# Down projection of a SwiGLU block: eleven instead of seven of 22 weight pairs with seven products, their sums made earlier and kept in DRAM

## Chip, core and metric

The kernel runs on one core of one Trainium2 chip. The metric is the device time of one execution in microseconds (us), as a median of the runs shown. Engines are named as in the profile: PE (TensorE matmul), PEld (TensorE weight load), DVE (VectorE), ACT (ScalarE), POOL (GpSimd), SP (SyncE, which issues most DMAs; SPq is its queue).

## The reference, cut to what matters

A decoder block for 256 tokens (and 16 meta tokens) of width 2048, all in float32. RWKV-7 time mixing, forgetting attention, their gates and the output projection come first and are not touched by the change. What matters here is the feed-forward part at the end, with `w_gu` of 2048 x 11264 and `w_dn` of 5632 x 2048:

```python
    h = h + merged @ w_o
    gate, up = jnp.split(_rms(h, n2) @ w_gu, 2, axis=-1)
    return h + (jax.nn.silu(gate) * up) @ w_dn
```

## The kernel before

**Precision.** Every float32 operand is split into a high and a low part in a 32-bit matmul format: the high part is a rounded copy that ACT makes, the low part is the difference that DVE makes. A product of two operands is three matmuls (high x high, low x high, high x low; `product`, L1457 to L1463, each 512 columns wide). The split is `split` (L509) for activations and `wload` (L314) for weights, whose ACT line is L335 and DVE line L336.

**Weight tiles.** Weights come from DRAM by DMA on SP's queue into a tile `raw` of 128 x 1024 float32 (512 KB). ACT and DVE then make `wh` and `wl` of it. There are four buffers of each (`RAWB = 4`, `WB = 4`, L49 and L50). So a DMA can be issued as soon as DVE has read the tile four places earlier, and ACT can write `wh` as soon as PE has used the one four places earlier. `run` (L426) writes each tile's load ahead of the matmuls of the tile before it, so SP, ACT and DVE run ahead of PE as far as these buffers let them.

**Planner.** Small work beside the matmuls is written as generators. `spawn` sets one off, `slot` (L397) advances a clock of estimated PE time with every product, and when a generator's time has come its next step is put into the program there; the number that a step yields is the time until the next one in ns. That sets the program order. In this last part of the kernel the framework's scheduler may move instructions of an engine against each other by its own estimates; data dependencies are kept by semaphores.

**Gate and up** (L1386 to L1404). For each of eleven blocks of 512 columns, 8 weight tiles for the gate and 8 for up: 176 tiles, each used by 8 pairs of matmuls (one of 512 columns, L441, one of 256, L443 or L440). `hts` holds the normalized activations, high and low. `post_gate` and `post_up` finish a block on ACT and DVE and leave silu(gate) * up in `ach` and `acl` (high and low), with hidden units on the partitions.

**Down projection** (L1410 to L1573). The 5632 rows of `w_down` make 22 pairs of two 128-row blocks. The output is computed in two column groups (`cg`) of 1024 columns; within one, a pair is a 2 x 2 block product: two token halves, two row blocks, two column halves of 512.
- A slow pair (`slow_jobs`, L1469) has two weight tiles of 512 KB and makes eight products, four a tile, so 24 matmuls. They add up in four PSUM banks `dn`.
- A fast pair (`fast_jobs`, L1488) makes seven products (21 matmuls) in Winograd's form of Strassen's method. Three of them, and one more factor, need sums of token blocks (`sst`, made by `sums_of_pairs`, L1417, with ten DVE operations and four splits a batch), and four need differences of weight blocks (L1515: four DVE operations of 128 x 512 a fast pair and column group, into `tt`). It loads 1 MB into two `raw` tiles (`ra`, `rb`, L1496 and L1498) and makes four steps of weights: a half tile for one product, then three whole tiles for two products each. Four of its sums stay in PSUM banks `dnp` over all fast pairs; `sums_of_products` (L1547) adds them to the output once per column group, and `post` (L1555) adds `dn` and stores the output.
- `ORDER` (L71) says in which order pairs run. With F for a fast pair and S for a slow one it is eight S and then (F S) seven times in the first column group; S F S seven times and one S in the second.

SP's queue takes the weight loads in this order; there is no work for POOL in gate and up or in the down projection.

## Time and profile before

| | us |
|---|---|
| median of 3 runs (lowest to highest) | 1522.12 (1520.21 to 1522.53) |
| span of the profiled execution, first to last instruction | 1517.7 |
| gate and up, matmuls from 788.8 to 1278.1 | 489 |
| down projection, first to last start of its matmuls, 1278.3 to 1513.5 | 235 |
| from there to the end of the span | 4 |

The span is 4.4 us shorter than the median; what lies around it the profile does not show. In the profile, a line such as L1460 is a line of the kernel; a group of instructions has its count, its busy time, the mean of one, and the idle time of its engine just ahead with what ended it. PE's busy time is pipelined: a matmul of 512 columns lasts 0.39 us, but the next starts 0.23 us after it. So PE can look busy throughout although it waits now and then; waits show in the starts.

### The profile page before, as it was taken

Reading aid. Unit: us, or ns where it says so; the run is one execution under the profiler, and the core shown is the slowest. Engines: PE = TensorE matmul, PEld = TensorE weight load, DVE = VectorE, ACT = ScalarE, POOL = GpSimd, SP = SyncE. Lnnn points to the kernel's source line nnn. Section 1 sums busy time; section 2 is a strip of 40 time slices with the busy share of each in tenths; the row PEclk is TensorE's granted clock in tenths of the full one; section 3 lists DMA queues with packets and bytes.
Section 4 is the critical chain, followed back from the end, with each engine's and each line's share of the span. In section 5 each row is a group of like instructions: output and inputs, shape, how many; then the busy total and the mean of one; then the engine's idle time right before and its main releaser. Section 6 shows DMA issues by size and latency. Waiting matters only on the chain.

```text
span 1517.7 us, 26174 instructions
## 1 busy us (share of the span) xinstructions
PE 1509.9 (99%) x10071; PEld 1339.5 (88%) x10071; DVE 1112.0 (73%) x2009; ACT 808.3 (53%) x1230; POOL 99.3 (7%) x182
## 2 busy tenths in 40 slices
PE   9999999999999999999999999999999999999998
PEld 9999999999989888998888888888888888887887
DVE  7888699689789857875665666566566658879776
ACT  7664565475465545644554555454455545554543
POOL 2112202202202000000000000000000000000000
PEclk9999999999999999999999999999999999999999
DMA  8557456646645757777566666666666666566664
GB/s 271 166 166 212 119 156 185 170 122 173 188 127 149 223 152 214 234 231 240 181 179 192 189 187 193 191 186 192 190 187 191 193 186 182 178 211 201 213 206 138
DMA packets 210365, 283.32 MB, mean 187 GB/s; under 512 B 24320, under 2 KB 129296, under 8 KB 210240
## 3 DMA queue, kind: packets, MB, share of 16 engines
q1 hardware_dynamic: 205344, 277.25, 61.9%
q10 hardware_dynamic: 4896, 4.40, 0.9%
q8 instruction: 79, 1.29, 0.3%
q14 instruction: 46, 0.38, 0.1%
HBM read 274.36 MB, written 7.24 MB: 186 GB/s over the span
## 4 chain that ended last, share of the span: by engine, by line
PE 95%; DVE 3%; DMA 1%; issue 1%; ACT 0%; SPq 0%; DVEq 0%; ACTq 0%
PE up L441 11%; PE gt L441 11%; PE zg L441 8%; PE gt L443 5%; PE up L443 5%; PE dn L1461 4%; PE dn L1460 4%; PE dn L1462 4%; PE zg L443 4%; PE f L441 2%; PE br L365 2%; PE br L366 2%; PE br L367 2%; PE f L365 2%; PE wo L1329 2%; PE wo L1331 2%
## 5 line engine op out<-in xcount | busy, mean ns | idle before, releaser
L336 DVE TENSOR_TENSOR wl<-raw,wh 128x1024 fp32r<-128x1024 f32 x460 | 561.9, 1226 | 281.3 <-ACT wh L335 280.6
L335 ACT ACTIVATE wh<-raw 128x1024 fp32r<-128x1024 f32 x460 | 486.5, 1059 | 470.2 <-PE up L441 118.9
L441 PE MATMUL gt<-hts,wh 128*128 128x512 f32 x704 | 242.9, 393 | 0.0
L441 PE MATMUL up<-hts,wh 128*128 128x512 f32 x704 | 242.7, 392 | 0.0
L443 PE MATMUL gt<-hts,wl 128*128 128x256 f32 x660 | 184.8, 280 | 0.0
L443 PE MATMUL up<-hts,wl 128*128 128x256 f32 x660 | 184.6, 280 | 0.0
L441 PE MATMUL zg<-xhl,wh 128*128 128x512 f32 x512 | 181.2, 399 | 0.0
L441 PEld LDWEIGHTS up<-hts,wh 128*128 128x128 f32 x704 | 130.0, 188 | 25.2
L441 PEld LDWEIGHTS gt<-hts,wh 128*128 128x128 f32 x704 | 129.9, 188 | 25.1
L443 PE MATMUL zg<-xhl,wl 128*128 128x256 f32 x480 | 134.3, 280 | 0.0
L443 PEld LDWEIGHTS up<-hts,wl 128*128 128x128 f32 x660 | 125.3, 190 | 1.8
L443 PEld LDWEIGHTS gt<-hts,wl 128*128 128x128 f32 x660 | 125.3, 190 | 1.8
L441 PEld LDWEIGHTS zg<-xhl,wh 128*128 128x128 f32 x512 | 94.3, 188 | 18.7 <-issue 0.7
L1460 PE MATMUL dn<-wh,ach 128*128 128x512 f32 x282 | 110.7, 393 | 0.0
L1461 PE MATMUL dn<-wh,acl 128*128 128x512 f32 x282 | 110.6, 392 | 0.0
L1462 PE MATMUL dn<-wl,ach 128*128 128x512 f32 x282 | 110.5, 393 | 0.0
L443 PEld LDWEIGHTS zg<-xhl,wl 128*128 128x128 f32 x480 | 90.9, 189 | 1.2
L365 PE MATMUL f<-xhl,wh 128*128 128x272 f32 x256 | 75.9, 296 | 0.0
L367 PE MATMUL f<-xhl,wl 128*128 128x272 f32 x256 | 73.6, 288 | 0.0
L366 PE MATMUL f<-xhl,wh 128*128 128x272 f32 x256 | 73.6, 288 | 0.0
L1462 PEld LDWEIGHTS dn<-wl,ach 128*128 128x128 f32 x282 | 52.9, 187 | 12.3 <-DVE wl L336 0.3
L1461 PEld LDWEIGHTS dn<-wh,acl 128*128 128x128 f32 x282 | 52.9, 188 | 12.0
(493 smaller groups left out, 3056.7 us busy)
## 6 DMA issues: line engine op xcount, KB each, us to landing
raw<-in_w_gate_up_dram SPq DMA_DIRECT2D x176, 512.0 KB, 4.3
raw<-in_w_in_dram SPq DMA_DIRECT2D x160, 512.0 KB, 3.9
raw<-in_w_down_dram SPq DMA_DIRECT2D x74, 512.0 KB, 5.0
raw<-in_w_o_dram SPq DMA_DIRECT2D x32, 512.0 KB, 4.3
raw<-in_w_branch_a_dram SPq DMA_DIRECT2D x16, 512.0 KB, 4.6
raw<-in_w_branch_b_dram SPq DMA_DIRECT2D x16, 512.0 KB, 5.0
raw<-in_w_down_dram SPq DMA_DIRECT2D x28, 256.0 KB, 4.6
zgd<-zg ACTq DMA_DIRECT2D x30, 128.0 KB, 3.8
```

The lines of the kernel that those rows point to most:

```text
L335: nc.scalar.activation(th, rr, AF.Copy)
L336: nc.vector.tensor_tensor(tl, rr, th.bitcast(F32), op=ALU.subtract)
L365: nc.tensor.matmul(ps, wh, ah, start=first, stop=False)
L366: nc.tensor.matmul(ps, wh, al, start=False, stop=False)
L367: nc.tensor.matmul(ps, wl, ah, start=False, stop=last)
L441: nc.tensor.matmul(ps.rearrange("p (a t) -> p a t", a=2), wh, act, start=first, stop=last)
L443: nc.tensor.matmul(ps[:, :T], wl, act[:, 0, :], start=False, stop=False)
L1329: nc.tensor.matmul(o, ah[:, kt, ts_], hi, start=first, stop=False)
L1331: nc.tensor.matmul(o, ah[:, kt, ts_], lo_, start=False, stop=last)
L1460: nc.tensor.matmul(o, a[0], hi, start=first, stop=False)
L1461: nc.tensor.matmul(o, a[1], hi, start=False, stop=False)
L1462: nc.tensor.matmul(o, a[0], lo_, start=False, stop=last)
```

## The change

Eleven pairs (0 to 10) are fast instead of seven. What a fast pair needs beside the weights themselves is made during gate and up:

- `sums_of_weights`, a planned step that starts after the first gate block: for each of the 11 fast pairs and each column group, POOL issues two DMAs of 512 KB that load the pair's two row blocks into `r`; 8.5 us of planned time later DVE makes the four differences in three operations into `v` (one of 128 x 1024, two of 128 x 512), and POOL issues a DMA of 1 MB that stores them in a DRAM tile `ts`; 10.5 us later comes the next one.
- `sums_of_tokens`: at the end of an up block, for each fast pair, DVE makes the four token sums in four operations of 128 x 128, and POOL stores them in DRAM (256 KB).
- In the down projection, `split_of_sums` loads the token sums back (11 DMAs of 256 KB on POOL's queue) and splits them in six batches, two splits each.
- A fast pair's four weight steps are now four loads of their own on SP's queue: 256 KB, two of 256 KB, 512 KB of `ts`, 512 KB of `ts`. It uses four `raw` tiles (1.75 MB) where it used two (1 MB). The four DVE operations of L1515 and `sums_of_pairs` are gone.
- The order is S S S S, (F F S) five times, F S S in the first column group; S, (F F S) five times, F S S S S S in the second.
- For room in SBUF, `hts` is kept with all high parts ahead of all low parts, the output projection's small tiles move to a pool that is closed after the first gate block, and `finish_job` is called ahead of the down projection.

```diff
+HPART = KT * T + NMETA
+HTS = 2 * HPART
...
-FAST = [0, 1, 2, 3, 4, 5, 6]
-BATCHES = (2, 2, 2, 1)
-SLOW = list(range(7, 22))
-ORDER = [SLOW[:8] + [i for pair in zip(FAST, SLOW[8:]) for i in pair],
-         [i for n, f in enumerate(FAST) for i in (SLOW[2 * n], f, SLOW[2 * n + 1])] + SLOW[14:]]
+FAST = list(range(11))
+BATCHES = (2, 2, 2, 2, 2, 1)
+SLOW = list(range(11, 22))
+
+
+def quick_and_plain(lead):
+    order = SLOW[:lead]
+    for n in range(0, len(FAST), 2):
+        order += FAST[n:n + 2] + SLOW[lead + n // 2:lead + n // 2 + 1]
+    return order + [i for i in SLOW if i not in order]
+
+
+ORDER = [quick_and_plain(4), quick_and_plain(1)]
+FETCHED = 8500
+STORED = 10500
 PAIRS = 5500
...
+    hts = ht.tile([P, HTS], F32R, tag="hts", name="hts")[:, :2 * HPART].rearrange("p (a e) -> p a e", a=2)
+    hts = hts[:, :, NMETA:].rearrange("p a (k t) -> p k a t", t=T)
...
+    tsd, ssd = {}, {}
+
+    def sums_of_weights():
+
+        for cg in range(2):
+            for i in FAST:
+                r = pre.tile([P, 2, 1024], F32, tag="r", name="r", bufs=1)
+                for k in range(2):
+                    nc.gpsimd.dma_start(r[:, k, :], wdn[i * 256 + k * P:i * 256 + (k + 1) * P, cg * 1024:(cg + 1) * 1024])
+                yield FETCHED
+                v = pre.tile([P, 2, 2, 512], F32, tag="v", name="v", bufs=1)
+                (b11, b12), (b21, b22) = ((r[:, k, :512], r[:, k, 512:]) for k in range(2))
+                nc.vector.tensor_tensor(v[:, 0], r[:, :, 512:], r[:, 0].rearrange("p (x c) -> p x c", x=2),
+                                        op=ALU.subtract)
+                nc.vector.tensor_tensor(v[:, 1, 0], b22, v[:, 0, 0], op=ALU.subtract)
+                nc.vector.tensor_tensor(v[:, 1, 1], b21, v[:, 1, 0], op=ALU.subtract)
+                d = tsd[i, cg] = dp.tile([P, 2, 1024], F32, tag=f"ts{i}{cg}", name=f"ts{i}{cg}")
+                nc.gpsimd.dma_start(d, v.rearrange("p n x c -> p n (x c)"))
+                yield STORED
+
+    def sums_of_tokens(i, u0, u1):
+
+        (a11, a21), (a12, a22) = ((u[:, :P], u[:, P:]) for u in (u0, u1))
+        sx = pre.tile([P, 4, P], F32, tag="sx", name=f"sx{i}", bufs=1)
+        for n, x_, y_, op in ((0, a21, a22, ALU.add), (1, sx[:, 0], a11, ALU.subtract), (2, a11, a21, ALU.subtract),
+                              (3, a12, sx[:, 1], ALU.subtract)):
+            nc.vector.tensor_tensor(sx[:, n], x_, y_, op=op)
+        d = ssd[i] = dp.tile([P, 4, P], F32, tag=f"ss{i}", name=f"ss{i}")
+        nc.gpsimd.dma_start(d, sx)
+
...
+            us = []
...
+                us.append(ub)
+                if m % 2 and 2 * j + m // 2 in FAST:
+                    sums_of_tokens(2 * j + m // 2, *us[m - 1:])
+        run(cm_jobs(wgu[:, j * 512:(j + 1) * 512], KT, hts, 0, T, post_gate, name=f"gt{j}"))
+        if j == 0:
+            wo_pool.__exit__(None, None, None)
+            pre = pre_pool.__enter__()
+            spawn(sums_of_weights(), HOP)
+        run(cm_jobs(wgu[:, DFF + j * 512:DFF + (j + 1) * 512], KT, hts, 0, T, post_up, alloc=aux_ps, name=f"up{j}"))
...
+    finish_job()
+    pre_pool.__exit__(None, None, None)
+    ht_pool.__exit__(None, None, None)
+    dn_pool = tc.tile_pool(name="dnp", bufs=1, reuse_waits="tile")
+    dn = dn_pool.__enter__()
+    sst = dn.tile([P, len(fast), 3, 2, P], F32R, tag="sst", name="sst")
+
+    def split_of_sums():
+
+        at, got = 0, []
         for n in BATCHES:
-            fs, ps_ = slice(at, at + n), slice(fast[at], fast[at] + n)
+            sl = dn.tile([P, 2, 4, P], F32, tag="sl", name=f"sl{at}", bufs=2)
+            for x_ in range(n):
+                nc.gpsimd.dma_start(sl[:, x_], ssd[fast[at + x_]])
+            got.append((at, n, sl))
             at += n
-            h = lambda k, t: acp_h[:, ps_, k, t, :].bitcast(F32)
-            l = lambda k, t: acp_l[:, ps_, k, t, :].bitcast(F32)
-            f = [sst[:, fs, i, 1, :] for i in range(3)] + [acp_l[:, ps_, 0, 1, :]]
-            hi = [sst[:, fs, i, 0, :] for i in range(3)] + [acp_h[:, ps_, 0, 1, :]]
-            f32 = [hp.tile([P, T], F32, tag="ga", name=f"s{at}{i}", bufs=8)[:, :n * P].rearrange("p (i c) -> p i c", c=P)
-                   for i in range(4)]
-
-            def tt(i, x_, y_, op):
-                nc.vector.tensor_tensor(f32[i], x_, y_, op=op)
-            tt(0, h(0, 1), h(1, 1), ALU.add)
-            tt(0, f32[0], l(0, 1), ALU.add)
-            tt(0, f32[0], l(1, 1), ALU.add)
-            tt(1, f32[0], h(0, 0), ALU.subtract)
-            tt(1, f32[1], l(0, 0), ALU.subtract)
-            tt(2, h(0, 0), h(0, 1), ALU.subtract)
-            tt(2, f32[2], l(0, 0), ALU.add)
-            tt(2, f32[2], l(0, 1), ALU.subtract)
-            tt(3, h(1, 0), f32[1], ALU.subtract)
-            tt(3, f32[3], l(1, 0), ALU.add)
             yield PAIRS
-            for i in range(4):
-                nc.scalar.activation(hi[i], f32[i], AF.Copy)
-                nc.vector.tensor_tensor(f[i], f32[i], hi[i].bitcast(F32), op=ALU.subtract)
-            yield PAIRS
+            for a_, n_, s_ in got:
+                fs, ps_ = slice(a_, a_ + n_), slice(fast[a_], fast[a_] + n_)
+                split(sst[:, fs, :, 0, :], sst[:, fs, :, 1, :], s_[:, :n_, :3])
+                split(acp_h[:, ps_, 0, 1, :], acp_l[:, ps_, 0, 1, :], s_[:, :n_, 3])
+            got = []
 
...
     def fast_jobs(i, cg, cs, ps, end):
-        box = {}
-
         def b(k, x_):
             return wdn[i * 256 + k * P:i * 256 + (k + 1) * P, cg * 1024 + x_ * 512:cg * 1024 + (x_ + 1) * 512]
 
+        def fresh():
+            return wp.tile([P, 1024], F32, tag="raw", name="raw", bufs=RAWB)
+
         def load0():
-            ra, rb = (wp.tile([P, 1024], F32, tag="raw", name="raw", bufs=RAWB) for _ in range(2))
-            nc.sync.dma_start(ra, wdn[i * 256:i * 256 + P, cg * 1024:(cg + 1) * 1024])
+            r = fresh()
+            nc.sync.dma_start(r[:, :512], b(0, 0))
+            w = split_tiles()
+            split(*(t[:, 0:2] for t in w), rows(r)[:, 0:2])
+            return w
+
+        def load1():
+            r = fresh()
             for x_ in range(2):
-                nc.sync.dma_start(rb[:, (1 - x_) * 512:(2 - x_) * 512], b(1, x_))
-            box["r"] = rows(ra), rows(rb)
+                nc.sync.dma_start(r[:, (1 - x_) * 512:(2 - x_) * 512], b(1, x_))
             w = split_tiles()
-            split(*(t[:, 0:2] for t in w), box["r"][0][:, 0:2])
+            split(*w, rows(r))
             return w
 
-        def load1():
-            w = split_tiles()
-            split(*w, box["r"][1])
-            return w
-
-        def load2():
-            (b11, b12), (b22, b21) = ([r[:, 0:2], r[:, 2:4]] for r in box["r"])
-            w, v = split_tiles(), split_tiles()
-            ts = [rows(hp.tile([P, 1024], F32, tag="tt", name="tt", bufs=2)) for _ in range(2)]
-            t1, t2, t3, t4 = (t[:, 2 * n:2 * n + 2] for t in ts for n in range(2))
-            for o, x_, y_ in ((t1, b12, b11), (t2, b22, t1), (t3, b22, b12), (t4, b21, t2)):
-                nc.vector.tensor_tensor(o, x_, y_, op=ALU.subtract)
-            split(*w, ts[0])
-            box["v"] = v, ts[1]
-            return w
-
-        def load3():
-            v, t = box["v"]
-            split(*v, t)
-            return v
+        def sums(n):
+            def load():
+                r = fresh()
+                nc.sync.dma_start(r, tsd[i, cg][:, n])
+                w = split_tiles()
+                split(*w, rows(r))
+                return w
+            return load
 
         first = i == fast[0]
 
@@ -1535,19 +1575,19 @@
 
         def mul2(w):
             product(ps[1], s_of(i, 0), w, 0, first, end)
-            product(ps[2], s_of(i, 1), w, 1, first, end)
+            product(ps[3], s_of(i, 2), w, 1, first, end)
 
         def mul3(w):
-            product(ps[3], s_of(i, 2), w, 0, first, end)
+            product(ps[2], s_of(i, 1), w, 0, first, end)
             product(cs[2], a_of(i, 1, 1), w, 1, False, False)
             if end:
                 sums_of_products(cg, ps)
-        return [(load0, mul0), (load1, mul1), (load2, mul2), (load3, mul3)]
+        return [(load0, mul0), (load1, mul1), (sums(0), mul2), (sums(1), mul3)]
 
...
-    spawn(sums_of_pairs(), 2 * PAIRS)
+    spawn(split_of_sums(), GAP)
```

More of the change, by code (lines that the diff above doesn't have):

```diff
@@ L1350, in post @@
                     nc.tensor.transpose(pt[:, t * P:(t + 1) * P], hh[:, t, k * P:(k + 1) * P], ident)
-                tmp = hp.tile([P, T], F32, tag="htmp", name=f"htmp{k}", bufs=3)
+                tmp = wo.tile([P, T], F32, tag="htmp", name=f"htmp{k}", bufs=3)
                 nc.vector.tensor_scalar(tmp, pt, vc("n2", k), None, op0=ALU.mult)
-                split(hts[:, k, 0, NMETA:], hts[:, k, 1, NMETA:], tmp)
+                split(hts[:, k, 0], hts[:, k, 1], tmp)
         run(tm_jobs(A["w_o"][0][:, js], KT, mgh, mgl, post, f"wo{j}"))
@@ L1359, in hybrid_block @@
     rsqrt_small(hp, rs2, ms2, [P, 2], "rst2")
-    obs = [hp.tile([P, P], F32, tag="ob", name=f"ob{t}", bufs=2) for t in range(2)]
+    obs = [wo.tile([P, P], F32, tag="ob", name=f"ob{t}", bufs=2) for t in range(2)]
     for t in range(2):
@@ L1380, in hybrid_block @@
     acp = ap_pool.__enter__()
+    pre_pool = tc.tile_pool(name="pre", bufs=1, reuse_waits="tile")
     NF = DFF // P
@@ L1384, in hybrid_block @@
     wgu = A["w_gate_up"][0]
+    wdn = A["w_down"][0]
+    tsd, ssd = {}, {}
[23 more added lines that the diff above has]
+        nc.gpsimd.dma_start(d, sx)
     for j in range(DFF // 512):
@@ L1400, in post_up @@
                 split(ach[:, 4 * j + m, :], acl[:, 4 * j + m, :], ub)
-        run(cm_jobs(wgu[:, j * 512:(j + 1) * 512], KT, hts, NMETA, T, post_gate, name=f"gt{j}"))
-        run(cm_jobs(wgu[:, DFF + j * 512:DFF + (j + 1) * 512], KT, hts, NMETA, T, post_up, alloc=aux_ps, name=f"up{j}"))
-    wdn = A["w_down"][0]
+                us.append(ub)
[7 more added lines that the diff above has]
+        run(cm_jobs(wgu[:, DFF + j * 512:DFF + (j + 1) * 512], KT, hts, 0, T, post_up, alloc=aux_ps, name=f"up{j}"))
     fast = FAST
@@ L1413, in hybrid_block @@
     acp_h, acp_l = (t.rearrange("p (i k) (t c) -> p i k t c", k=2, t=2) for t in (ach, acl))
-    sst = hp.tile([P, KT, 2, L], F32R, tag="hts", name="sst").rearrange("p k a t -> p (k a t)")
-    sst = sst[:, :len(fast) * 6 * P].rearrange("p (i s a c) -> p i s a c", i=len(fast), s=3, a=2)
-    def sums_of_pairs():
-        at = 0
+    finish_job()
[3 more added lines that the diff above has]
+    dn = dn_pool.__enter__()
@@ L1572, in hybrid_block @@
     finish_job()
+    dn_pool.__exit__(None, None, None)
     hp_pool.__exit__(None, None, None)
```

11 lines of the change are left out of this document (7 added, 4 removed).

## The prediction

> **What bounds the kernel now.** I read the page first: its span, busy times, chain and DMA issues.
>
> ```profile
> span 1517.7 us, 26174 instructions
> PE 1509.9 (99%) x10071; PEld 1339.5 (88%) x10071; DVE 1112.0 (73%) x2009; ACT 808.3 (53%) x1230; POOL 99.3 (7%) x182
> ...
> PE 95%; DVE 3%; DMA 1%; issue 1%; ACT 0%; SPq 0%; DVEq 0%; ACTq 0%
> ...
> L336 DVE TENSOR_TENSOR wl<-raw,wh 128x1024 fp32r<-128x1024 f32 x460 | 561.9, 1226 | 281.3 <-ACT wh L335 280.6
> L335 ACT ACTIVATE wh<-raw 128x1024 fp32r<-128x1024 f32 x460 | 486.5, 1059 | 470.2 <-PE up L441 118.9
> L441 PE MATMUL gt<-hts,wh 128*128 128x512 f32 x704 | 242.9, 393 | 0.0
> ...
> L441 PE MATMUL zg<-xhl,wh 128*128 128x512 f32 x512 | 181.2, 399 | 0.0
> ...
> raw<-in_w_gate_up_dram SPq DMA_DIRECT2D x176, 512.0 KB, 4.3
> raw<-in_w_in_dram SPq DMA_DIRECT2D x160, 512.0 KB, 3.9
> raw<-in_w_down_dram SPq DMA_DIRECT2D x74, 512.0 KB, 5.0
> ...
> raw<-in_w_down_dram SPq DMA_DIRECT2D x28, 256.0 KB, 4.6
> ```
>
> PE carries 95% of the chain: a matmul less is time gained, if weights keep coming. The last column of the DMA rows is the median time from issue to landing, and it differs by stage. So the next view is the busy time by stage, gate and up in the first row, down projection in the second; behind it the down projection's matmuls by tile, with first and last start.
>
> ```profile
> 790.00:1278.00 488.00, 488.00 (x2818) 430.52 (x2817) 305.62 (x461) 245.66 (x355) 0.00 (x0) 1.00 0.66 190
> 1278.00:1516.00 238.00, 235.12 (x1018) 189.96 (x1016) 191.87 (x253) 118.90 (x136) 0.00 (x0) 1.00 0.60 191
> ```
> ```profile
> L1460 PE MATMUL dn<-wh,ach x282: 387/392/399, 1278.3 to 1513.0; 128*128 128x512 f32 x141
> ...
> L1462 PE MATMUL dn<-wl,ach x282: 391/392/501, 1278.8 to 1513.5; 128*128 128x512 f32 x141
> ```
> ```profile
> L1460 PE MATMUL dnp<-wh,sst x42: 390/394/498, 1324.6 to 1501.3; 128*128 128x512 f32 x42
> ...
> L1460 PE MATMUL dnp<-wh,ach x14: 392/392/397, 1322.5 to 1497.8; 128*128 128x512 f32 x14
> ```
>
> In the first view the columns after the length are PE, PEld, DVE, ACT, POOL, granted clock, share of the DMA engines, GB/s. POOL does nothing in either stage, and DMA is at 0.66 and 0.60. Where PE waits in the down projection, and how fast it goes when it doesn't:
>
> ```profile
> SPq L326 <- DVE wl L336: 59.0, 30, 6.2
> ```
> ```profile
> PEld dnp L1460 <- ACT wh L510: 1.2, 2, 1.0
> PEld dnp L1462 <- DVE wl L511: 1.1, 2, 0.6
> ...
> PEld dn L1462 <- DVE wl L336: 0.3, 1, 0.3
> ```
> ```profile
> 1361.22 0.39 PE L1460 MATMUL dn<-wh,ach 128*128 128x512 f32 x1
> 1361.45 0.40 PE L1461 MATMUL dn<-wh,acl 128*128 128x512 f32 x1
> 1361.68 0.39 PE L1462 MATMUL dn<-wl,ach 128*128 128x512 f32 x1
> ```
>
> Waits for weights come to 1.2 + 1.1 + 0.3 = 2.6 us. The 1014 matmuls (three lines of 282 + 42 + 14) start over 1513.5 - 1278.3 = 235.2 us, so one takes (235.2 - 2.6)/1013 = 0.230 us, as the three starts show.
>
> **Fewer matmuls.** Four more fast pairs in two column groups make one product, three matmuls, less each: 4 x 2 x 3 = 24, times 0.230 = 5.5 us off PE's path. That seven products stand where eight stood can be counted in the code, so that the change doesn't do what it says is no rival. The end stays as it is: a slow pair, its additions, its stores.
>
> **Weights for the down projection.** This is the term that decides. SP waited 59 us there for a `raw` tile to be read by DVE, so the four `raw` buffers already set when a load starts. A tile's turn in its buffer is landing, ACT, DVE; four turns run at once. Two more rows give the half tile:
>
> ```profile
> L511 DVE TENSOR_TENSOR wl<-raw,wh 128x512 fp32r<-128x512 f32 x14 | 9.6, 687 | 1.2 <-ACT wh L510 0.9
> ```
> ```profile
> L510 ACT ACTIVATE wh<-raw 128x512 fp32r<-128x512 f32 x14 | 8.9, 635 | 15.9 <-PE dn L1461 10.2 <-DMA raw<-in_w_down_dram 4.0 <-PE dnp L1461 1.7
> ```
> ```profile
> 1326.44 1.51 SPq L326 DMA_DIRECT2D raw<-in_w_down_dram  x2
> ...
> 1330.52 0.82 SPq L1498 DMA_DIRECT2D raw<-in_w_down_dram  x2
> ...
> 1380.03 1.51 SPq L326 DMA_DIRECT2D raw<-in_w_down_dram  x2
> ```
>
> - A whole tile: 5.0 + 1.06 + 1.23 = 7.3 us. The half tile of a fast pair: 4.6 + 0.64 + 0.69 = 5.9. Its second tile, two DMAs of 256 KB, the second issued 0.41 us later (0.82/2): 0.4 + 4.6 + 2.3 = 7.3. The two tiles of differences: 7.3 each, with the 512 KB row for want of one of their own.
> - F F S: 2 x (5.9 + 3 x 7.3) + 2 x 7.3 = 70.2 us of turns, over four buffers 17.5 us. PE needs 21 + 21 + 24 = 66 matmuls, 15.2 us. Short by 2.4 us.
> - F S: 42.4/4 = 10.6 against 45 x 0.230 = 10.35. Short by 0.25 us.
> - Five F F S and one F S in a column group: 5 x 2.4 + 0.25 = 12.2 us; both groups 24.4 us.
> - Against it stands what slow pairs lay by: four tiles of a slow pair last 4 x 4 x 3 x 0.230 = 11.0 us, a turn 7.3, so loads come 3.7 us early. Each group starts from slow pairs, so I take this off once a group: 24.4 - 7.4 = 17.0 us. That split weights lie ready ahead of PE as well I don't count: that lead is in tiles, and shrinks with them.
>
> Two things in the profile bear this out. In the F S part of before the loads of the slow pair come every (1380.03 - 1326.44)/5 = 10.72 us, more than PE's 10.35: supply is short there already, and from it come most of the 2.6 us. (There DVE's differences hold `raw` too; that goes with the change.) And F F S moves 2 x 1.75 + 1 = 4.5 MiB, 4.72 MB, in 15.2 us: 310 GB/s, where 191 GB/s took a share of 0.60, so the share would be 0.97.
>
> The bounds are the landing times. With 3.9 us (the `w_in` row) F F S is 59.2/4 = 14.8 us, nothing is short, and the term is 0. With 6.3, the longest median of a 512 KB load,
>
> ```profile
> hh<-in_x_dram SPq DMA_DIRECT2D x4, 512.0 KB, 6.3
> ```
>
> F F S is 83.2/4 = 20.8 us and F S 12.5, short by 30 us a group, about 55 in all. I take the `w_down` row itself, 5.0: same tensor, same buffers. 5.3 would give 26 us, 4.6 some 5 us.
>
> A rule of the Trainium skill differs here: "DMA: Bandwidth & Descriptors", in its anatomy of one DMA, fits a DMA's time as about 2.0 us plus bytes over 436 GB/s. As an estimate by that page 512 KB land in 3.2 us, F F S is not short, and the whole comes to 1514.0 us. The rows above, 3.9 to 5.0, are all longer, and they decide.
>
> **What leaves DVE, ACT and SP in the down projection.** Per fast pair four operations of L1515 go, and `sums_of_pairs`; for six batches of two splits come two ACT and two DVE operations each, spread over the first 30 us and needed from 4 x 5.5 = 22 us on. DVE is then at 2 x (0.69 + 3 x 1.23) + 2 x 1.23 = 11.2 of 15.2 us in F F S, so neither DVE nor ACT is the bound. I cost it at 0; if the first splits come late, it is up to 2 us. SP issues five DMAs a fast pair instead of three, 5 x 0.41 = 2.1 of 4.8 us; a later load queues behind one that waits, as before. The load of `ts` waits for its store, which landed long ago for all but the last.
>
> **What gate and up take on.** Per fast pair and column group: two loads of 512 KB, a store of 1 MB, DVE operations of 1.23 + 2 x 0.69 = 2.6 us; per fast pair four token sums and a store of 256 KB. On DVE 22 x 2.6 = 57 us and 44 x 0.29 = 13 us:
>
> ```profile
> L1431 DVE TENSOR_TENSOR s<-s,acl 128x128 f32<-128x128 f32 x6 | 1.6, 288 | 0.1
> ```
>
> That makes 376 of 488 us. Its cover is seen in the timeline of a steady stretch:
>
> ```profile
> 1039.82 1.06 ACT L335 ACTIVATE wh<-raw 128x1024 fp32r<-128x1024 f32 x1 [1.71 <-PE up L441]
> ...
> 1042.59 1.06 ACT L335 ACTIVATE wh<-raw 128x1024 fp32r<-128x1024 f32 x1 [1.71 <-PE up L441]
> ```
> ```profile
> 1040.91 1.23 DVE L336 TENSOR_TENSOR wl<-raw,wh 128x1024 fp32r<-128x1024 f32 x1 [1.55 <-ACT wh L335]
> ```
>
> A tile comes every 2.77 us and ACT waits for PE to free a buffer. So three tiles, 8.3 us, lie ready when a split of 2.3 us begins: 6.0 us of lead. And DVE frees `raw` at 1042.1, its next load lands 4.3 us later, at 1046.4, and ACT takes it at 1039.8 + 4 x 2.77 = 1050.9: 4.5 us more. The added wait is DVE's for `r`; behind it in DVE's order stand the next `wl`, and PE waits for those once 6.0 us are gone. The step leaves 8.5 planned us for it. On POOL's queue the store waits for DVE and the next load stands behind it; nothing else is there.
>
> No row of before shows a DMA issued by POOL. In bytes: 22 x 2.1 + 11 x 0.26 = 49 MB in 488 us, 100 GB/s beside 190. By the gate and up row the DMA share would be 0.66 x 290/190 = 1.01, by the down row 0.60 x 290/191 = 0.91. Close to full, but with 10 us of lead for every burst. I take 0 for the stage, not below, since its matmuls stay, and carry the rest as a rival. The other layout of `hts` I cost at 0: gate and zg matmuls read tiles of different shape at 393 and 399 ns.
>
> **Sum.** 1517.7 - 5.5 - 2.6 + 17.0 = 1526.6 us of span; the median is 4.4 us above the span, so **1531.0 us**.
>
> **Rivals.**
> - *Supply holds* (faster). Landing stays under 4.6 us. For it: the loads come one by one where before issued them in pairs, and rows of the differences are 4 KB long. Against: DMA is much fuller. Then 1517.7 - 8.1 + 4.4 = 1514.0, up to 1519 with 5 us of waits. Chance 0.27; the skill's fit above would lead here.
> - *The two cancel*: waits of 5 to 11 us, 1519 to 1525. Chance 0.11.
> - *Gate and up become DMA-bound* (slower too). A round of `sums_of_weights` is 19 planned us, 20.6 real ones; the stage's own loads need 0.66 x 20.6 = 13.6 of them, so POOL's 2.1 MB may take 7.0. At 190/0.66 = 288 GB/s they take 7.3. If stores cost more, say 8 us, it is 22 x 1.0 less 10 of lead: 12 more, 1542, and more beyond. Chance 0.14. Here the same page of the Trainium skill speaks against the change: by its section "Issuing engines are not separate DMA queues", DMAs of GpSimd and Sync run on the same 16 engines and interleave, so another queue brings no bandwidth; no run here shows it yet.
>
> **How the numbers follow.** The forecast, waits of over 11 us in the down projection, has 0.48, with a range of its own of 1525 to 1545 (waits from 11 us, and the 26 us of a landing of 5.3 with 5 for the rest). About 0.2%, 3 us, can be told from no change. Faster 0.27, same 0.11, slower 0.48 + 0.14 = 0.62. The range 1515 to 1546 leaves out the lowest of the first rival (0.05), the upper half of the third (0.07) and the forecast's tail (0.06).
>
> **What would show it.** Right: 990 matmuls between the stage's first and last start, 240 us or more instead of 235; PE's waits for `wl` and `wh` in F F S; loads of two rounds of F F S about 17 us apart and not 15.2; landing of the `w_down` loads at 5 us or more; gate and up within 1 us of 489. Wrong: landings near 4.3 us and a stage of 228 us; or PE waiting during gate and up, with DVE waiting for `r`.

## The result, and the profile after

The changed kernel takes 1595.23 us (median of 5 runs, 1594.31 to 1598.85) against 1522.12 (5 runs, 1519.67 to 1522.53): ratio 1.0494, 95% interval 1.0483 to 1.0505, so 73 us slower. The forecast was 1531.0, 9 us slower, with 1546 as its upper end.

The page of the changed kernel, its span, the chain and the DMA issues (median us from issue to landing at the end of a row):

```profile
span 1592.6 us, 26485 instructions
...
PE 66%; DMA 13%; issue 10%; DVE 8%; ACT 2%; POOL 1%; SPq 0%; DVEq 0%; ACTq 0%; POOLq 0%
...
raw<-in_w_gate_up_dram SPq DMA_DIRECT2D x176, 512.0 KB, 5.3
...
r<-in_w_down_dram POOLq DMA_DIRECT2D x44, 512.0 KB, 9.4
ts<-v POOLq DMA_DIRECT2D x22, 1024.0 KB, 6.7
raw<-in_w_down_dram SPq DMA_DIRECT2D x44, 512.0 KB, 5.9
raw<-ts SPq DMA_DIRECT2D x44, 512.0 KB, 5.8
raw<-in_w_down_dram SPq DMA_DIRECT2D x66, 256.0 KB, 4.2
```

PE carried 95% of the chain before and carries 66% now; DMA and DVE have come in. Where this is, two views tell: the last starts of matmuls in gate and up and in the down projection, and the busy time by stage (PE, PEld, DVE, ACT, POOL, granted clock, DMA share, GB/s).

```profile
L454 PE MATMUL up<-hts,wh x704: 387/395/495, 812.5 to 1320.1; 128*128 128x512 f32 x176
```
```profile
L1506 PE MATMUL dn<-wh,ach x242: 387/394/628, 1320.3 to 1587.7; 128*128 128x512 f32 x121
...
L1508 PE MATMUL dn<-wl,ach x242: 387/392/628, 1320.8 to 1588.1; 128*128 128x512 f32 x121
```
```profile
790.00:1320.00 530.00, 506.19 (x2820) 436.69 (x2819) 358.40 (x557) 242.85 (x355) 43.32 (x81) 0.99 0.81 269
1320.00:1590.00 270.00, 246.16 (x994) 183.18 (x992) 170.07 (x183) 133.75 (x149) 3.75 (x7) 0.99 0.73 238
```

Gate and up start at 789.1 us and end at 1320.1: 531.0 us instead of 489.3, 41.7 more, where the forecast had 0. By PE's starts 26.9 of it are waits (starts 0.45 us or more apart, less 0.23 each and less the 0.7 of before); 13.7 us of the stage run at a granted clock of 0.50, which costs 6.8; and outside both a matmul takes 176.1 ns on average from start to start instead of 173.5, 7.3 us over 2816 of them. The down projection lasts 1588.1 - 1320.3 = 267.8 us instead of 235.2, 32.6 more, where it had 8.9. Together 74.3 of the span's 74.9.

What the engines wait for in gate and up (us in total, times, longest), and the difference rounds on DVE and POOL in the timeline:

```profile
ACT wh L348 <- DMA raw<-in_w_gate_up_dram: 139.3, 67, 7.2
DVE v L1417 <- DMA r<-in_w_down_dram: 78.4, 17, 6.5
...
PE gt L456 <- DVE wl L349: 19.8, 11, 3.8
```
```profile
1074.33 1.23 DVE L1417 TENSOR_TENSOR v<-r 128x1024 f32<-128x1024 f32 x1 [4.39 <-DMA r<-in_w_down_dram]
...
1089.77 1.22 DVE L1417 TENSOR_TENSOR v<-r 128x1024 f32<-128x1024 f32 x1 [5.28 <-DMA r<-in_w_down_dram]
```
```profile
1078.55 0.54 POOL L1422 DMA_DIRECT2D ts<-v  x1 [13.73 <-DVE v L1420]
1079.35 1.05 POOL L1413 DMA_DIRECT2D r<-in_w_down_dram  x2 [0.26 <-issue]
```

Three things are to be seen. This round comes 15.4 us after the last, not 20.6. DVE stands still 4 to 5 us for `r` in most rounds, and the weight splits stand behind it. And POOL issues the next two loads 0.8 us after the store: 2 MB set off at once, although 10.5 planned us lie between them. The planner's time says where an instruction stands in the program; POOL has nothing else to do, so they keep no time between the store and the next load.

In the down projection PE's own waits and those of its weight loads:

```profile
ACT wh L523 <- DMA raw<-ts: 35.7, 29, 3.1
ACT wh L523 <- DMA raw<-in_w_down_dram: 32.9, 19, 4.6
PEld dnp L1508 <- DVE wl L524: 21.1, 27, 1.0
...
PEld dnp L1506 <- ACT wh L523: 14.1, 15, 1.8
```

### The profile page after: what moved, and what is told of

It reads as the page before. It is cut to its first block, busy times and chain, and to the rows that moved or that the text cites. A ratio compares the mean times of both kernels' runs of the same rounds, so it can differ in the third digit from the quotient of the medians.

```text
span 1592.6 us, 26485 instructions
## 1 busy us (share of the span) xinstructions
PE 1538.4 (97%) x10047; PEld 1337.9 (84%) x10047; DVE 1141.5 (72%) x2035; ACT 819.4 (51%) x1242; POOL 149.8 (9%) x270
## 4 chain that ended last, share of the span: by engine, by line
PE 66%; DMA 13%; issue 10%; DVE 8%; ACT 2%; POOL 1%; SPq 0%; DVEq 0%; ACTq 0%; POOLq 0%
PE zg L454 8%; PE up L454 5%; PE gt L454 5%; DMA r<-in_w_down_dram 4%; DMA raw<-in_w_down_dram 4%; PE zg L456 4%; DMA raw<-ts 3%; DVE wl L349 3%; PE up L456 2%; PE gt L456 2%; PE f L454 2%; PE br L378 2%; PE br L379 2%; PE br L380 2%; PE f L378 2%
## 5 line engine op out<-in xcount | busy, mean ns | idle before, releaser
L348 ACT ACTIVATE wh<-raw 128x1024 fp32r<-128x1024 f32 x444 | 469.2, 1059 | 482.8 <-DMA raw<-in_w_gate_up_dram 139.3
L349 DVE TENSOR_TENSOR wl<-raw,wh 128x1024 fp32r<-128x1024 f32 x444 | 540.7, 1225 | 185.6 <-ACT wh L348 183.0
L454 PE MATMUL gt<-hts,wh 128*128 128x512 f32 x704 | 252.3, 401 | 0.0
L456 PE MATMUL gt<-hts,wl 128*128 128x256 f32 x660 | 190.1, 288 | 20.1 <-DVE wl L349 19.8
L524 DVE TENSOR_TENSOR wl<-raw,wh 128x512 fp32r<-128x512 f32 (+1 forms) x88 | 95.0, 1090 | 76.3 <-ACT wh L523 71.7
L523 ACT ACTIVATE wh<-raw 128x512 fp32r<-128x512 f32 (+1 forms) x88 | 82.6, 950 | 90.7 <-DMA raw<-ts 35.7
L1508 PE MATMUL dn<-wl,ach 128*128 128x512 f32 x242 | 97.0, 401 | 4.1 <-DVE wl L524 2.6
L1506 PE MATMUL dn<-wh,ach 128*128 128x512 f32 x242 | 96.7, 400 | 0.4 <-ACT wh L523 0.4
L1507 PE MATMUL dn<-wh,acl 128*128 128x512 f32 x242 | 96.0, 397 | 0.0
L1417 DVE TENSOR_TENSOR v<-r 128x1024 f32<-128x1024 f32 x22 | 26.9, 1224 | 78.4 <-DMA r<-in_w_down_dram 78.4
```

The lines of the kernel that those rows point to most:

```text
L348: nc.scalar.activation(th, rr, AF.Copy)
L349: nc.vector.tensor_tensor(tl, rr, th.bitcast(F32), op=ALU.subtract)
L454: nc.tensor.matmul(ps.rearrange("p (a t) -> p a t", a=2), wh, act, start=first, stop=last)
L456: nc.tensor.matmul(ps[:, :T], wl, act[:, 0, :], start=False, stop=False)
L523: nc.scalar.activation(hi, src, AF.Copy)
L524: nc.vector.tensor_tensor(lo_, src, hi.bitcast(F32), op=ALU.subtract)
```

## Experiments

Theory of the forecast: PE waits for weights in the down projection because four `raw` buffers turn too slowly. After the result a second was needed for gate and up; the candidates were the bytes, DVE's work, the order of the differences on DVE, the bursts on POOL's queue, and the layout of `hts`. Before took 1519.9 to 1520.6 us beside these runs; each experiment is one run but where an interval is given. "Gate and up" and "down" are first to last start of their matmuls, as above. Runs whose code for a stage is the same differ all the same where PE waits a lot: gate and up take 531.0, 533.9 and 536.6 us in after, e10_sixraw_half and e7_sixraw, the down projection 263.8 to 268.6 in after, e1_later, e2_nodiff, e8_nodiff_sx and e11_queued. Differences of a few us between single runs of such stages say little.

| run | us | gate and up | down |
|---|---|---|---|
| before | 1522.12 | 489.3 | 235.2 |
| after | 1595.23 | 531.0 | 267.8 |
| e1_later | 1592.36 | 532.5 | 265.1 |
| e2_nodiff | 1626.42 | 566.8 | 264.7 |
| e3_notraffic | 1560.95 | 494.7 | 271.3 |
| e8_nodiff_sx | 1556.15 | 497.6 | 263.8 |
| e11_queued | 1579.75 | 516.2 | 268.6 |
| e14_inplace | 1566.14 | 501.7 | 269.8 |
| e6_fly10 | 1530.36 | 497.6 | 238.1 |
| e12_fly10_old | 1524.24 | 490.2 | 239.8 |
| e7_sixraw | 1576.06 | 536.6 | 244.5 |
| e10_sixraw_half | 1561.77 | 533.9 | 232.9 |
| e15_repaired | 1542.71 | 498.1 | 248.3 |
| e17_repaired_sx | 1537.65 | 495.4 | 247.6 |
| e13_fly9_old | 1525.20 | 490.2 | 239.8 |
| e16_fly9_late | 1515.90 | 490.2 | 231.8 |

### Gate and up: planned times, DVE's work, bytes

**e1_later** gives the loads of `r` more planned time: `FETCHED = 14000`, `STORED = 5000`.

> The step that takes the differences comes 14.0 instead of 8.5 planned us after its loads, and the next round 5.0 instead of 10.5 us after that, so rounds and traffic stay. If DVE's wait for r (78 us in 17 waits, longest 6.5) holds up the weight splits behind it, gate and up fall from 531 to about 490 us and the kernel to about 1553. If full DMA engines are the cause (weights of the stage landing at 6.0 instead of 4.3 us, up to 11), DVE's wait goes but the stage stays over 515 us.

Nothing moves. One tile's rows say why, `v` in the kernel after and then here (durations, first and last start):

```profile
L1417 DVE TENSOR_TENSOR v<-r x22: 1218/1226/1227, 813.0 to 1170.0; 128x1024 f32<-128x1024 f32 x22
```
```profile
L1417 DVE TENSOR_TENSOR v<-r x22: 1215/1224/1228, 812.4 to 1171.5; 128x1024 f32<-128x1024 f32 x22
```

Twenty-one rounds in 357 and in 359 us, 17 us each where 20.6 were planned. In DVE's order mostly 5 or 6 weight splits stand between two rounds in both kernels; 20.6 us are 7 to 8 of them, and e11_queued below, which pins the differences to their place in the program, has 7 or 8. So the framework's scheduler had moved the differences ahead, and a planned time doesn't bind it.

**e2_nodiff** leaves out the differences on DVE and stores `r` as it is:

```diff
-                nc.vector.tensor_tensor(v[:, 0], r[:, :, 512:], r[:, 0].rearrange("p (x c) -> p x c", x=2),
-                                        op=ALU.subtract)
...
-                nc.gpsimd.dma_start(d, v.rearrange("p n x c -> p n (x c)"))
+                nc.gpsimd.dma_start(d, r)
```

> The three DVE operations that take the weight differences are left out and POOL stores the loaded weights themselves, so the output is not the reference's; loads, stores and their times of issue stay. If DVE's in-order wait is the cause, gate and up take about 490 us; if the traffic is, they stay over 515 us.

Less work, 36 us more. The row that explains it:

```profile
DVE sx L1425 <- DMA ss<-sx: 90.5, 5, 20.9
```

The store of the token sums stands on POOL's queue behind the store of `r`, which now waits there for its load; `sx` has one buffer, so DVE waits up to 20.9 us for it, with the weight splits behind. The experiment made a wait of its own and told nothing of DVE's work. **e8_nodiff_sx** mends it with `bufs=5` for `sx`, the differences still left out.

> As e2_nodiff, and the token sums have five buffers instead of one, so DVE no longer waits there for POOL's queue. The differences are left out and the loaded weights stored, so the output is not the reference's. All of POOL's traffic stays, at e2's pace or faster. If the traffic by itself is harmless and DVE's wait for r was the cause, gate and up take 489 to 497 us; if full DMA engines are the cause, over 515 us.

```profile
810.00:1100.00 290.00, 290.00 (x1646) 252.14 (x1645) 184.56 (x299) 144.21 (x208) 33.12 (x62) 1.00 0.93 325
```

All the bytes are there, DMA is at 0.93 and 325 GB/s, PE is busy for 290.00 of 290.00 us, and its starts show no wait. So the bytes alone don't make PE wait. (The stage's 497.6 us are those of e6_fly10 below, which has no differences at all: the layout.) But the run takes away more than DVE's wait. With one buffer for `r`, the store waits for its load and the next load for the store, so the two are never in flight together as they are in after:

```profile
906.28 0.54 POOL L1416 DMA_DIRECT2D ts<-r  x1 [6.98 <-DMA r<-in_w_down_dram]
914.23 1.05 POOL L1413 DMA_DIRECT2D r<-in_w_down_dram  x2 [7.41 <-DMA ts<-r]
```

The Trainium skill's "DMA: Bandwidth & Descriptors", section "Issuing engines are not separate DMA queues", says that DMAs run on the same 16 engines whichever engine issues them. The trace agrees: their share is 0.93 here and 0.66 in before. But that was not the loss.

**e3_notraffic** keeps the differences on DVE and leaves out POOL's loads and stores of them (the operands are a tile set to 1.0; the down projection loads rows of `w_down` in place of `ts`).

> POOL's loads and stores of the weight differences are left out; DVE makes the same operations on a tile that was set once, and the down projection loads weights of the same size in place of the differences, so the output is not the reference's. Whether the wait or the traffic is the cause, gate and up go back to 489 to 492 us. If they stay over 500, DVE's added 57 us of work are the cause, which both theories exclude.

```profile
PE up L456 <- DVE wl L349: 0.4, 1, 0.4
```

That is PE's only wait in the stage. So DVE's 57 us alone don't do it either. (Of the 5.4 us above before, 4.8 come from starts that follow each other more slowly without a wait: the layout, below.) What is left is the two together: DVE waiting in its order for late data, which the next two runs take apart. The down projection is as long as in after, so `ts` as a source isn't what slows it.

### Gate and up: order and bursts

**e11_queued** pins each difference behind the weight split that precedes it in the program:

```diff
-            nc.vector.tensor_tensor(tl, rr, th.bitcast(F32), op=ALU.subtract)
+            last["wl"] = nc.vector.tensor_tensor(tl, rr, th.bitcast(F32), op=ALU.subtract)
...
+                with tc.issue_after(last["wl"].ins):
```

> The three difference operations are queued on DVE behind the weight split that stands where the plan put them, so a round takes 7.5 splits (20.6 us), as planned, and not the 5.4 (15 us) that the scheduler made of it; nothing else changes. If the scheduler's early place for operations that wait for r is the cause, DVE's wait for r falls from 78 to under 15 us, gate and up from 531 to 490 to 500, the kernel to about 1555. If the burst of a store and two loads at once is, landings of the stage's own loads stay at 8 to 11 us during it and the stage stays over 510.

```profile
L1420 DVE TENSOR_TENSOR v<-r x22: 1216/1219/1222, 818.5 to 1287.9; 128x1024 f32<-128x1024 f32 x22
```

Rounds are 22.4 us apart, DVE no longer waits for `r`, and the stage is 14.8 us shorter. PE's waits by its starts fall from 26.9 to 13.0 us. But POOL still issues store and loads back to back, and the stage's own loads land late:

```profile
raw<-in_w_gate_up_dram SPq DMA_DIRECT2D x176, 512.0 KB, 8.0
```

**e14_inplace** makes the differences in `r` itself, in four operations, so the next loads can't start until the store has read it:

```diff
-                v = pre.tile([P, 2, 2, 512], F32, tag="v", name="v", bufs=1)
...
+                    for o, x_, y_ in ((b11, b12, b11), (b12, b22, b12), (b22, b22, b11), (b21, b21, b22)):
+                        nc.vector.tensor_tensor(o, x_, y_, op=ALU.subtract)
...
+                nc.gpsimd.dma_start(d, r)
```

> e11_queued with the differences made in place: r is overwritten by them, v is gone, so the next loads can't start until the store has read r, and store and loads are no longer in flight together. New layout of hts kept. Theory A, what is left of the loss in gate and up of e11_queued (516 us) is bursts of 2 MB on POOL's queue plus 8 us of layout: the stage takes 497 to 501 us, the loads of w_gate_up land in 6 to 7 us. Theory B, it is the bytes or the DVE operations: the stage stays at 512 us or more. Down projection as in the kernel after, 266 to 269 us.

```profile
1000.12 0.54 POOL L1422 DMA_DIRECT2D ts<-r  x1 [9.29 <-DVE r L1420]
1007.42 1.06 POOL L1415 DMA_DIRECT2D r<-in_w_down_dram  x2 [6.76 <-DMA ts<-r]
```
```profile
raw<-in_w_gate_up_dram SPq DMA_DIRECT2D x176, 512.0 KB, 6.5
```

The loads now come 7.3 us after the store. Landing falls from 8.0 to 6.5 us, the stage by another 14.5 to 501.7: nearer to theory A by far, 0.7 above its upper end. Not all of the 14.5 is the burst: PE's waits fall by 7.5 us to 5.5 and its time at half the clock from 13.7 us to 3.4, worth 5.1, but some 2.7 us come from starts that follow each other faster where nothing waits (next section). (The 5.3 of the kernel after is no better than these: its rounds were over at 1173 us, and its median takes in the 147 us of undisturbed loads behind them.)

### Gate and up: the layout

**e6_fly10** has the token sums by way of DRAM and the new layout, but no differences in DRAM: ten fast pairs, whose differences are made in the down projection as in before, slow pairs between all of them.

> One part alone: token sums made during gate and up and kept in DRAM as in the change, but ten fast pairs whose weight differences DVE makes in the down projection as before, with one slow pair after each fast one. No POOL traffic but 20 transfers of 256 KB. By the turn of the buffers gate and up stay within 2 us of 489 (both causes named there are absent), and the down projection has 18 matmuls less than before, 4.1 us, against supply that is short by 0.37 us for a fast and a slow pair, 7 us over 20 of them, less what slow pairs lay by: 233 to 240 us, so 1516 to 1525 in all. If fast pairs as such starve PE whatever their traffic, over 250.

PE never waits in gate and up and has a clock of 1.00, yet the stage takes 497.6 us, against the expectation. **e12_fly10_old** is the same kernel with the layout of before:

```diff
-    hts = ht.tile([P, HTS], F32R, tag="hts", name="hts")[:, :2 * HPART].rearrange("p (a e) -> p a e", a=2)
-    hts = hts[:, :, NMETA:].rearrange("p a (k t) -> p k a t", t=T)
+    hts = ht.tile([P, KT, 2, L], F32R, tag="hts", name="hts")[:, :, :, NMETA:]
```

> e6_fly10 with hts in the layout of before (high and low part of each row block side by side). In e6_fly10 PE never waited in gate and up and the clock was 1.00, yet the stage took 497.6 us instead of 489.3. Theory A, the layout slows every pair of matmuls by 6 ns: the stage is back at 489 to 490 us and a pair starts every 340 ns instead of 346; the total is 1522 to 1524. Theory B, the token sums' stores or their DVE operations do it: the stage stays at 497 to 498 us and the total at 1530.

The same 100 us of both, e6_fly10 first; the number behind PE's busy time is that of its matmuls:

```profile
1100.00:1200.00 100.00, 100.00 (x569) 86.99 (x568) 61.20 (x92) 50.21 (x74) 0.00 (x0) 1.00 0.59 185
```
```profile
1100.00:1200.00 100.00, 100.00 (x578) 88.05 (x577) 64.69 (x100) 50.75 (x74) 0.00 (x0) 1.00 0.65 188
```

569 against 578 matmuls with PE busy throughout in both: 1.6%, 7.4 us over the stage; a pair starts every 353 ns instead of 348. Theory A holds for these two kernels. But the price is no constant of the layout. e3_notraffic has the new layout too, and changes its pace within the stage:

```profile
850.00:950.00 100.00, 100.00 (x569) 86.92 (x568) 95.44 (x144) 49.10 (x71) 2.16 (x4) 1.00 0.61 195
```
```profile
1100.00:1200.00 100.00, 100.00 (x575) 87.76 (x574) 62.88 (x95) 50.11 (x75) 0.00 (x0) 1.00 0.60 189
```

e14_inplace, with this layout, also starts 575 matmuls from 1100 to 1200 us, e15_repaired, with the old one, 578. Why PE is slower with the new layout, and what sets by how much, is open; it wasn't tried further.

### Down projection: buffers and bytes

**e7_sixraw** gives a fast pair's first tile and its second tile of differences two buffers of their own, in place of which the token sums come back one pair at a time:

```diff
+            if more:
+                return dn.tile([P, 1024], F32, tag="rawd", name="rawd", bufs=2)
...
-            r = fresh()
+            r = fresh(True)
...
-                r = fresh()
+                r = fresh(n == 1)
```

> In the down projection the first and the last tile of a fast pair get two buffers of their own, so six tiles can be under way instead of four (the token sums are split one pair at a time for room). If the turn of four buffers sets the pace (landing plus 2.3 us, four at once), the two rings need 13.6 and 11.7 us for two fast pairs and a slow one against PE's 15.2, and the stage falls from 268 to 228 to 238 us, the kernel to about 1560. If the rate of the DMA engines sets it (310 GB/s wanted, 238 measured over the stage), landing times rise instead and the stage stays over 255 us.

**e10_sixraw_half** is e7_sixraw with half the bytes of each `ts` tile loaded and used twice, so that two of a fast pair's products are made of the wrong factors.

> As e7_sixraw, and of each difference tile only half is loaded, used twice, so the output is not the reference's; the number of loads, the buffers, and ACT's, DVE's and PE's work stay, and 21 MB of the down projection's 63 go by half (22 x 2 x 0.25 MB less). If what e7 left (244.5 us against 228) is the rate of the DMA engines, the stage falls to 228 to 234 us. If it is something else (DVE, ACT, the early token sums), it stays above 240.

PE's waits for DVE's and ACT's halves of the weights, first e7_sixraw, then e10_sixraw_half:

```profile
PE dnp L1508 <- DVE wl L524: 4.5, 9, 0.5
PE dnp L1506 <- ACT wh L523: 3.7, 5, 1.2
```
```profile
PE dnp L1508 <- DVE wl L524: 1.0, 2, 0.5
...
PE dnp L1506 <- ACT wh L523: 0.7, 1, 0.7
```

990 matmuls need 990 x 0.230 = 227.7 us. Of the 40.1 us above that in after, two more buffers take 23.3, and fewer bytes 11.6 more; 5.2 are left. The 244.5 us of e7_sixraw lie between its two forecasts. The turn of the buffers is the larger part: the 512 KB loads land only a little earlier than in after (5.1 to 5.8 us instead of 5.8 and 6.0). What the bytes do is less clear. With half of them the loads of `ts` land in 3.8 and 4.4 us, so the buffers turn faster too, and e10_sixraw_half can't tell the rate of the DMA engines from the turn.

### All of it together, and a kernel ahead of before

**e15_repaired** is e14_inplace with the old layout and the six buffers; **e17_repaired_sx** adds `bufs=4` for `sx` and puts the first split of the token sums later.

> e14_inplace with the old layout of hts and the two extra buffers of e7_sixraw, so all four causes undone, eleven fast pairs and differences in DRAM kept. If they add up: gate and up 489 to 493 us, down projection 244 us as in e7_sixraw, total 1527 to 1532, still behind before by the 9 us or so by which the down projection is longer. If there is one cause more, the total is over 1540.

> e15_repaired with four buffers instead of one for the token sums in gate and up, and the first split of the sums later, as in e16_fly9_late. In e15_repaired PE waited 7.1 us in five places of gate and up; ahead of the last of them DVE waited 6.0 us for the store of the earlier token sums to free the one buffer. Theory A, that buffer is what is left: the stage falls from 498.1 to 490 to 493 us and the total to 1534 to 1538. Theory B, it is the loads on the 16 engines at 300 GB/s: the stage stays at 496 us or more. The down projection loses up to 4 us of its 248.3 if the first split matters here too.

In e15_repaired the layout is worth only 501.7 - 498.1 = 3.6 us, as the 575 against 578 matmuls above would have it; PE's waits are a little longer (7.1 us by its starts, instead of 5.5), and the 3.4 us at half the clock are gone. The causes don't add up to the end. e15_repaired is 11 us above the 1532 expected, and e17_repaired_sx still 17 behind before: 6 of it in gate and up, of which PE's starts show 4.5 as waits, and 12 in the down projection. The stage's 495.4 us lie between the two forecasts: the single `sx` buffer may have been 2.7 us, which one run of each can't settle. What makes the rest of the waits in gate and up stays open, and so does whether the 248 us that six buffers leave here differ from the 244.5 of e7_sixraw by more than such runs do.

**e13_fly9_old** is the other way out: nine fast pairs, no differences in DRAM, token sums by way of DRAM, a fast pair's first tile in two buffers of its own.

> Nine fast pairs whose differences are made in the down projection as before, token sums by way of DRAM, the old layout of hts, and the first weight tile of a fast pair in two buffers of its own. 1014 - 2 x 2 x 3 = 1002 matmuls in the down projection, 230.5 us of them at 0.230. If the buffers' turn was what the down projection waited for in e6_fly10 (238.1 us with 996 matmuls, 9 us of waits), the stage takes 231 to 233 us and the total is 1517 to 1519, ahead of before by 2 to 4 us. If it is the landing of the loads, the stage takes 235 to 237 us and the total is 1521 to 1523.

Ratio 1.0031 (1.0019 to 1.0043): not ahead, and 239.8 us are above both forecasts. Most of the loss is at one place, seen in ACT's timeline and then PE's:

```profile
1287.85 0.53 ACT L524 ACTIVATE sst<-sl 128x384 fp32r<-128x384 f32 x1 [4.91 <-DMA sl<-ss]
```
```profile
1293.36 0.80 PE L1489 MATMUL dn<-wl,ach 128*128 128x512 f32 x1 [3.14 <-DVE wl L350]
1293.96 0.63 PE L1487 MATMUL dn<-wh,ach 128*128 128x512 f32 x1
1294.38 0.63 PE L1488 MATMUL dn<-wh,acl 128*128 128x512 f32 x1
...
1299.08 0.47 PE L1487 MATMUL dn<-wh,ach 128*128 128x512 f32 x1
1299.38 0.40 PE L1488 MATMUL dn<-wh,acl 128*128 128x512 f32 x1
```

ACT waits in its order for the first token sums, PE runs dry for 3.1 us, and then starts a matmul every 0.43 us for 5.1 us. By the starts that is 6.1 us in all. **e16_fly9_late** puts that split later and pins it behind the weight splits, with four slow pairs ahead of the first fast one:

```diff
-            yield PAIRS
+            yield PAIRS if at > n else 3 * PAIRS
...
+                with tc.issue_after(last["wh"].ins), tc.issue_after(last["wl"].ins):
```

> e13_fly9_old lost its time at one place: ACT waited 4.9 us in its order for the first token sums to come back from DRAM (1282.9 to 1287.9 us), PE then waited 3.3 us at 1293 us and started its next 12 matmuls every 0.43 us instead of 0.23; from 1340 us on it started 218 matmuls in 50 us, so hardly waited. Here the first split of the token sums is placed 16.5 us into the stage instead of 5.5, behind a weight split, and four slow pairs lead instead of three. Theory A, that one wait and the slow matmuls behind it are the loss: the down projection falls from 239.8 to 231 to 234 us, the total to 1516 to 1519, ahead of before. Theory B, the wait only moves to the first fast pair: the total stays at 1522 to 1525.

1515.90 us (7 runs) against 1520.42: ratio 0.9970, interval 0.9959 to 0.9982, ahead of both kernels. 1002 matmuls instead of 1014, and hardly a wait:

```profile
L1490 PE MATMUL dn<-wh,ach x262: 391/394/401, 1278.7 to 1510.1; 128*128 128x512 f32 x131
```
```profile
PE dnp L1492 <- DVE wl L527: 0.7, 1, 0.7
```

## Why the prediction was wrong, point by point

The direction was right, and so was the mechanism in the down projection, at too small a size. What made the forecast miss is gate and up. The prediction named the sign for that itself: PE waiting there, with DVE waiting for `r`.

- **Fewer matmuls, 5.5 us**: right. 990 are there instead of 1014, and e16_fly9_late, with 1002 and hardly a wait, takes 3.4 us less in the stage than before, 2.8 for its 12 matmuls.
- **"What gate and up take on ... I take 0 for the stage"**: the step that failed, with 41.7 us. It set 10 us of lead against a planned 8.5 us for the load of `r`. But the scheduler didn't keep the planned order (e1_later, e11_queued: 14.8 us), and the step on POOL's queue said that the next load stands behind the store, without drawing the consequence: both go out at once (e14_inplace: 14.5 us, some 2.7 of them not the burst's). `r` landed in 9.4 us and the stage's own loads late with it. The two leads, DVE's 6.0 and the landing's 4.5, were counted one after the other; that the same burst used up both fits these rows, but no run shows it by itself. With both undone PE still waits 5.5 us (e14_inplace), and the rest is the layout and half the clock behind waits, which the sum had at nothing.
- **"The other layout of `hts` I cost at 0"**: wrong by 7.4 us (e6_fly10, e12_fly10_old), and by 7.3 in after by its starts. The rows for it, 393 and 399 ns, compared durations, which overlap in a pipelined PE; starts show the pace, and the layout of this very tile was in no row.
- **Weights for the down projection, +17.0**: right in kind, wrong in size. The sum went by landings of 5.0 and 4.6 us; they came to 5.9, 5.8 and 4.2. With these, by the same steps, a fast pair's turns are 5.5 + 6.9 + 2 x 8.1 = 28.6 us and a slow pair's 16.4, F F S needs 18.4 us instead of 15.2, F S 11.25 instead of 10.35, a group falls 16.9 short less 2.8 of lead: 28 us. Starts more than 0.45 us apart cost 30 us beyond their 0.23. The other 10 us are a term that the sum lacked: 63 starts of 0.30 to 0.45 us, 42 of them right behind a longer one, cost 7.0, and 14 starts at half the clock 2.8.
- **The 2.6 us of waits that go**: read from PEld's rows; PE's starts in before show 1.7. Nothing of it was gained, with the waits above in their place.
- **The rival "gate and up become DMA-bound"**, at 12 us: right in place, wrong in mechanism. (Its 12 us on top of 1531.0 are 1543, not 1542.) The share rose to 0.81, and with all the bytes at 0.93 PE doesn't wait (e8_nodiff_sx). The price was late landing and DVE's wait for it, not the rate.
- **The supply rival and the estimate of 3.2 us for 512 KB by the Trainium skill's fit**: the medians were 5.8 and 5.9 us, so the rows were the better guide, and still too low. The page, "DMA: Bandwidth & Descriptors", gives this fit in its section "Anatomy of one DMA — SWDGE (gpsimd) path", so for DMAs that GpSimd issues, and these are SP's; the 512 KB loads on POOL's queue took 9.4 us, two at a time.
- **First splits that come late, up to 2 us**: under-sized in e13_fly9_old, where that one wait, with the slow matmuls behind it, cost 6.1 us of the 8.0 between 239.8 and 231.8. In after ACT waited 7.2 us for token sums between 1332 and 1343 us; what of PE's waits behind it this made, no run shows.
- **The 4.4 us from span to median**: 2.6 in after. The time of an execution is 1.7 to 2.1 us above its own span in these runs (1594.31 over 1592.6), so part of the 4.4 was the spread between executions.

## What to carry to other kernels

A step put into the program at a planned time keeps that time only if something pins it there and if its queue has other work in between: look in the trace for the order on the engine and for a store and the next load issued together. An engine that works in order passes on any wait, so a new load needs the lead of everything behind its reader, and two leads that the same burst uses up count once. Price a fuller DMA by the landing times of a full stretch, and a new tile layout by the starts of its matmuls.

## What the runs showed of the hardware

- A wait costs PE more than itself. The start behind a wait is followed by the next after some 0.33 us instead of 0.23 (1355.63 to 1355.96 below). And the clock can be halved. In e13_fly9_old matmuls after 3.1 us of waiting start 0.43 us apart instead of 0.23 for 5.1 us, with a granted clock of 0.50:

```profile
1292.40:1299.20 6.80, 5.84 (x14) 4.59 (x15) 6.54 (x10) 1.67 (x3) 1.09 (x2) 0.50 0.72 225
```

The Trainium skill, "TensorE: Matmul & The Clock Gate", section "Part 1: The HAM clock gate", gives half the clock after an idle window of about 3.4 us. The half is in the trace; the wait was a little shorter than that. In the down projection of after no single wait was longer than 1.3 us, and it happened all the same:

```profile
1355.63 0.50 PE L1506 MATMUL dnp<-wh,sst 128*128 128x512 f32 x1 [1.34 <-ACT wh L523]
1355.96 0.40 PE L1507 MATMUL dnp<-wh,sst 128*128 128x512 f32 x1
1356.89 0.63 PE L1508 MATMUL dnp<-wl,sst 128*128 128x512 f32 x1 [0.53 <-DVE wl L524]
1357.31 0.63 PE L1506 MATMUL dn<-wh,ach 128*128 128x512 f32 x1
```
```profile
1357.10:1360.50 3.40, 3.40 (x9) 2.62 (x9) 2.88 (x3) 1.57 (x2) 0.00 (x0) 0.50 0.65 193
```

- DMA runs at 325 GB/s and a share of 0.93 for 290 us without a wait on PE, where POOL's loads and stores take turns and DVE has no differences to make (e8_nodiff_sx). At 269 GB/s and 0.81, with store and loads sent off together and DVE waiting for them, PE waits 26.9 us (after). Taking turns alone isn't enough: in e14_inplace, with the differences on DVE, PE still waits 5.5 us.
- The order of high and low parts of a matmul's operand in SBUF was worth 1.6% of PE's pace between e6_fly10 and e12_fly10_old (569 and 578 matmuls in 100 us), and 0.5% between e14_inplace and e15_repaired (575 and 578).
